# The feed-forward layers of a two-layer encoder in float32r: later sends, two swapped products, a later SiLU

## The chip, the cores and the metric

The kernel runs on one core of one Trainium2 chip, as one program. The metric is the device time of an execution in microseconds; the time of the kernel before is the median of three runs. The profile comes from one further execution, taken by the hardware profiler.

## The reference

The whole trunk of an encoder is computed for 1024 positions of width 1024: a gated delta-rule layer, a feed-forward layer, a chunked attention layer that reads a shared key and value, a second feed-forward layer, and a last norm. The change touches only the two feed-forward layers:

```python
FFN_DIM = 2816
FFN_CONV = 3

def conv_ffn(xn, w_up, conv_w, conv_b, w_down):
    h = causal_dwconv(xn @ w_up, conv_w) + conv_b
    gate, val = h[..., :FFN_DIM], h[..., FFN_DIM:]
    return (jax.nn.silu(gate) * val) @ w_down
...
h = h + conv_ffn(rmsnorm(h, f_norm[layer]), f_w_up[layer], f_conv[layer], f_conv_b[layer], f_w_down[layer])
```

## The kernel before

**Float32 from two halves.** A float32 operand is cut into a rounded high part and the rest. ScalarE (ACT) rounds (`cut_high`, L1434: tiles `uh`, `dh`, `eh`), and GpSimd (POOL) or VectorE (DVE) subtracts to get the low part (`cut_low`, L1412: `ul`, `dl`, `el`). A product of two such operands is three matmuls (`triple`: L1446 high by high, L1447 and L1448 with a low part of one side). A step of the program is one product of four `triple`s: twelve matmuls of 128x512.

**Seven products for eight.** Both matrix products are computed two by two blocks at a time by a scheme with seven block products in place of eight, so VectorE also makes sums of blocks of weights (`r<-r,r`, `ay<-a,a`) and of activations. The hidden width is 22 tiles of 128 for the gate and 22 for the value. Tile `j` of the first matrix takes the products `(j, n)` with `n` from 1 to 7, which write a PSUM bank `pu`. Products 1 and 2 of a tile share a bank: after `(j, 1)` ScalarE copies the bank to `keep` (L1575), and `(j, 2)` accumulates into the same bank. The x operands are `xh` and `xl` (products 1, 2, 3), `x7`, `xt2` (product 6), `xt1` (product 5) and `xt4`. Tile 0 is computed by eight plain products.

**The second matrix** takes the hidden tiles two at a time, in nine groups `g` of seven products, `second(g, n)`, in the order n = 1, 2, 5, 3, 6, 7, 4, one for every two products of the first matrix. Each writes two PSUM banks `pd`. `drain(g, n)` takes the banks out: by ScalarE copies to tiles `stage` (L1802), or for n = 6, 7 by VectorE sums onto the stage of products 3 and 5. `send(g, n)` (L1817) then adds the two stage tiles to a sum in device memory by two accumulating DMAs that GpSimd issues; products 3 and 5 have no send of their own. Product 1 goes to a shared sum `d_e`, which belongs into three of the four quarters. At the end of a layer `load_e` fetches the shared sum, half `u` at a time, and `send_e(u, n)` (L1824) adds it to the quarters of n = 6, 7 and 4.

**Convolution.** `taps` applies three taps per tile: step 0 on ScalarE (L1538), steps 1 and 2 on VectorE (L1541). `silu(j)` (L1544) is ScalarE's, `gated(j)` is VectorE's product with the value.

**What sets the order.** Within `ffn` nothing is scheduled by a tool: the order of instructions on every engine is written out. `step` appends a product to the list `seq`. `at(i, f, rank)` hangs a job on step `i`; before each step its jobs are run in order of rank, and what they issue stands in this order on each engine's queue.

```python
for i in range(len(seq) + 8):
    for _, f in sorted(jobs.pop(i, ()), key=lambda j_: j_[0]):
        f()
    if i < len(seq):
        seq[i]()
```

An operand of the first matrix is cut two steps ahead of its product (rank 1 where no other is given; on POOL where no engine is given). The weights of the second matrix are cut three steps ahead with rank 1.2, its hidden tiles with 1.4. The table `H` holds steps and ranks for the start of a layer: `first` is the order of the first 15 products behind tile 0, and `conv` gives step and rank of the taps, the SiLU (`s`) and the gated product (`m`) of tiles 0 to 2.

Of the kernel before, what the change touches and what calls it, by code (L numbers as in the profile page):

```python
# [28 lines left out]
def trunk_kernel(  # L29
# [25 lines left out]
    o = 0  # L55
# [452 lines left out]
    with ExitStack() as ph:  # L508
# [137 lines left out]
        def heads(t):  # L646

            return t // 2, range(4 * (t % 2), 4 * (t % 2) + 4)
# [602 lines left out]
        h, late = [], None  # L1251
# [92 lines left out]
        xh, xl = act_tiles()  # L1344
# [6 lines left out]
        with tc.manual_schedule(engines={mybir.EngineType.PE, mybir.EngineType.DVE, mybir.EngineType.Activation}):  # L1351
# [4 lines left out]
            for t in range(4):  # L1356
                s, hds = heads(t)
# [49 lines left out]
    def ffn(layer, h, hp, xs, tail, d_r, last):  # L1407
# [16 lines left out]
        H = {'cut': ({(0, 1): (0, 0), (1, 0): (1, 0), (1, 1): (1, 1)}, {(0, 1): (0, 0), (1, 0): (0, 0), (1, 1): (1, 0)}), 'c0': ({(0, 0): 'gg', (0, 1): 'av', (1, 0): 'av', (1, 1): 'ag'}, {(0, 0): 'gg', (0, 1): 'gg', (1, 0): 'gg', (1, 1): 'ag'}), 'x': {('s', 7): (5, 1), ('h', 7): (6, 1.306), ('s', 6): (5, 1.466), ('h', 6): (6, 2.01), ('l', 7): (7, 2.004), ('l', 6): (7, 2.612), ('s', 5): (9, 2), ('h', 5): (9, 2.01), ('l', 5): (10, 2.406), ('s', 4): (11, 2), ('h', 4): (11, 2.918), ('l', 4): (12, 1.039)}, 'xl': {7: (), 6: (), 5: (), 4: ()}, 'beats': ({(0, 2): 1, (1, 0): 20}, {(1, 3): 1, (2, 0): 20}), 'first': [(1, 1), (1, 2), (2, 1), (1, 7), (2, 2), (1, 6), (1, 5), (2, 7), (1, 4), (1, 3), (2, 6), (2, 5), (2, 4), (2, 3), (3, 1)], 'o': (2, 3, 5, 7, 7, 9, 11), 'ops': {(3, 3): (0.5, 2.5, 'v'), (3, 4): (1, 2, 'v'), (3, 2): (0.5, 1.12, 'v'), (1, 3): (1.1, 3, 'v'), (2, 7): (1, 3, 'g'), (2, 6): (1.1, 2.5, 'g'), (1, 5): (1, 1.3, 'v'), (3, 7): (0.5, 1.7, 'v'), (2, 1): (0.5, 2.5, 'v'), (3, 5): (1, 3, 'g'), (3, 6): (1.1, 1.12, 'g')}, 'conv': {0: {'g0': (11, 3.208), 'v0': (12, 1.815), 'v1': (13, 2), 'v2': (14, 2.418), 'g1': (14, 0.401), 'g2': (15, 2.01), 's': (16, 0.011), 'm': (17, 2)}, 1: {'v0': (18, 1.304), 'v1': (18, 1.468), 'v2': (19, 2), 'g0': (19, 0.403), 'g1': (20, 0.913), 'g2': (21, 0.903), 's': (22, 1.6), 'm': (23, 1.311)}, 2: {'v0': (22, 1.164), 'v1': (25, 1.805), 'v2': (25, 2), 'g0': (24, 2.606), 'g1': (26, 0.906), 'g2': (27, 0.408), 's': (28, 1.6), 'm': (30, 1.805)}}, 'gp': {1: (18, 1.807), 2: (24, 1.602)}, 'mix': (0, 1)}  # L1424

        seq, jobs = [], {}

        def at(i, f, rank=1):

            jobs.setdefault(max(i, 0), []).append((rank, f))  # L1430

        def cut_high(src, ring, copy=nc.scalar.copy):
            hi, lo = [(wd if ring == "e" else wf).tile([P, HALF], F32R, name=ring + x, tag=ring + x, bufs=RINGS[ring]) for x in "hl"]
            copy(hi, src)  # L1434
            return hi, lo
# [9 lines left out]
        def triple(ps, w, x, cw, first, last):  # L1445
            mm(ps, w[0][:, cw], x[0], start=first, stop=False, skip_group_check=True)  # L1446
            mm(ps, w[0][:, cw], x[1], start=False, stop=False, skip_group_check=True)  # L1447
            mm(ps, w[1][:, cw], x[0], start=False, stop=last, skip_group_check=True)  # L1448
# [62 lines left out]
        def operand(j, n, lo=True):  # L1511
# [110 lines left out]
        def plain(i):  # L1622
            def f():
# [18 lines left out]
        due = {}  # L1642
        for c, (j, n) in enumerate(plan):
# [65 lines left out]
        v0, v1, v2, g0, g1, g2 = [(v, i) for v in (1, 0) for i in range(3)]  # L1709
# [60 lines left out]
        def channels(g, n):  # L1770
            b11, b12, b21, b22 = [conv_t[2 * g + k, 1][:, hs(s)] for k in range(2) for s in range(2)]
            if n == 5:
                tt(nc.vector, b11, b12, b11, sub)
            elif n == 6:
                tt(nc.vector, b11, b22, b11, sub)
            elif n == 7:
                tt(nc.vector, b12, b22, b12, sub)
            elif n == 4:
                tt(nc.vector, b21, b21, b11, sub)
            src = {1: b11, 2: b21, 5: b11, 3: b22, 6: b11, 7: b12, 4: b21}[n]  # L1780
            bops[g, n] = cut_high(src, "e")
# [24 lines left out]
        def total(n, u):  # L1806
            if n == 1:
                return d_e[u]
            c, s = where[n]
            return d_c[c, s, u]  # L1810

        def send(g, n):
            for u in range(2):
                if g == 0 and (layer == 1 or n == 1):
                    nc.sync.dma_start(out=total(n, u), in_=stage[g, n, u])
                else:
                    nc.gpsimd.dma_start(out=total(n, u), in_=stage[g, n, u], accum_op=add)  # L1817
# [5 lines left out]
        def send_e(u, n):  # L1823
            nc.gpsimd.dma_start(out=total(n, u), in_=stage["e", u], accum_op=add)  # L1824

        for g in range(NG):
            p_ = {n: pos["d", g, n] for n in ORDER}
            b_ = {n: pos["d", g - 1, n] for n in ORDER} if g else {1: p_[1] - 4, 3: p_[1] - 4, 7: p_[1] - 4, 4: p_[1] - 3}
            for q, n in ((11, 7), (12, 3), (21, 7), (22, 4)):
                at(b_[n] - 2, lambda g=g, q=q: load_a(g, q), 3 + q / 100)  # L1830
            for n in ORDER:
                if n == 3:

                    def third(g=g):
                        low = channels(g, 3)
                        weights(g, 3, low)

                    at(p_[n] - 3, third, 1.2)
                else:
                    at(p_[n] - 3, lambda g=g, n=n: weights(g, n), 1.2)  # L1840
                    at(p_[n] - 3, lambda g=g, n=n: channels(g, n), 1.4)
                at(p_[n] + 1, lambda g=g, n=n: drain(g, n), 0)
                if n not in (3, 5):
                    at(p_[n] + 2, lambda g=g, n=n: send(g, n), 0.5)

        for u, i in ((0, pos["d", NG - 1, 5]), (1, fin_at + 2)):
            at(i, lambda u=u: load_e(u), 3)
            for k, n in enumerate((6, 7, 4)):
                at(i + 2 + k // 2, lambda u=u, n=n: send_e(u, n), 0.6)


        k0 = 2 * NG
# [25 lines left out]
        for q in range(8):  # L1878
            i = (fin_at + 1, fin_at + 1, pos[FP - 2, 6], pos[FP - 2, 7], pc[0], pc[3], pc[1], pc[1])[q]
# [59 lines left out]
        else:  # L1939
# [108 lines left out]
            i = 8  # L2048
# [34 lines left out]
    xh, xl = xb  # L2083
# [7 lines left out]
    first = two_tiles([load_w(w_kv, 0, fold=g_kv, on_act=True), load_w(b_w_q, 0, fold=g_b, on_act=True)], tail0, next_tile)  # L2091
# [5 lines left out]
    with ExitStack() as ph:  # L2097
# [354 lines left out]
        h, tails = [], []  # L2452
# [271 lines left out]
```

## Time and profile before

| | |
|---|---|
| median of 3 runs | 2499.43 us (2498.5 to 2502.1) |
| span of the profiled execution, first to last instruction | 2493.3 us |
| median less the span | 6.1 us |
| PE (matmuls) busy | 2466.1 us, 99% of the span |
| DVE, POOL, ACT busy | 1842.5, 1523.0, 1442.1 us |
| first feed-forward layer | about 643 to 1295 us |
| second feed-forward layer | about 1833 to 2480 us |

Matmul rows overlap: a row lasts 0.39 us, and the next one begins 0.23 us after the last began. So the busy share says little, and a loss is read from the starts of two successive matmuls, less 0.23 us each. The profiled execution has a span alone and no device time of its own beside it; the median of the runs shown is 6.1 us over this span.

### The profile page before, as it was taken

To read this page: it belongs to the slowest core of one execution; us is meant where nothing else is said; L and a number is where in the kernel's file an instruction comes from. 1 tells how busy PE (TensorE), PEld (TensorE's weight loads), DVE (VectorE), ACT (ScalarE), POOL (GpSimd) and SP (SyncE) were. 2 spreads that over 40 slices of the span, in tenths; PEclk is the share of its full clock that TensorE was granted. 3 is DMA by queue.
4 is the path that set the end of the run, shared out by engine and by line. 5 is a ranking of instruction groups with operands and counts; after the bars stand their busy time and mean duration, and the time that the engine had idled before them with its cause. 6 is when DMAs were issued, how large, how long until landed. Compare 5 with 4: busy or idle time off the path is not lost.

```text
span 2493.3 us, 39279 instructions
## 1 busy us (share of the span) xinstructions
PE 2466.1 (99%) x13785; PEld 2057.0 (83%) x13785; DVE 1842.5 (74%) x2985; ACT 1442.1 (58%) x2770; POOL 1523.0 (61%) x1548
## 2 busy tenths in 40 slices
PE   8999999999999999999999999999999999999998
PEld 6888888888888888888788888888877888888877
DVE  5665874567798888888866656666589788888886
ACT  6444546474465556565555666667456565666555
POOL 3655653357357777777626454455554777778774
PEclk9999999999999999999999999999999999999999
DMA  8734435565347777777841232333444799777788
GB/s 228 188 105 118 142 110 153 156 194 163 96 108 148 150 153 151 153 144 156 183 151 55 67 80 77 81 76 95 145 114 119 184 176 180 166 169 171 152 187 224
DMA packets 383877, 353.19 MB, mean 142 GB/s; under 512 B 97600, under 2 KB 304448, under 8 KB 383680
## 3 DMA queue, kind: packets, MB, share of 16 engines
q1 hardware_dynamic: 350704, 243.46, 34.4%
q0 software_dynamic: 28224, 98.58, 22.5%
q10 hardware_dynamic: 4752, 8.65, 0.9%
q8 instruction: 108, 1.77, 0.3%
q14 instruction: 89, 0.73, 0.1%
HBM read 182.25 MB, written 156.30 MB: 136 GB/s over the span
## 4 chain that ended last, share of the span: by engine, by line
PE 81%; POOL 6%; DVE 4%; issue 4%; DMA 2%; ACT 2%; SPq 0%; ACTq 0%; POOLq 0%; DVEq 0%
PE acc L118 8%; PE pu L1448 8%; PE acc L119 8%; PE acc L120 8%; PE pu L1446 8%; PE pu L1447 8%; PE pd L1448 3%; PE pd L1446 3%; PE pd L1447 3%; POOL ul L1412 3%; PE acco L118 2%; PE acco L120 2%; PE acco L119 2%; PE ptp L2353 2%; PE poT L2399 1%
## 5 line engine op out<-in xcount | busy, mean ns | idle before, releaser
L1412 POOL TENSOR_TENSOR ul<-r,uh 128x512 fp32r<-128x512 f32 x266 | 430.4, 1638 | 258.3 <-ACT uh L1434 253.5
L118 PE MATMUL acc<-xh,whi 128*128 128x512 f32 x896 | 369.3, 413 | 0.5 <-ACT xh L1094 0.5
L119 PE MATMUL acc<-xl,whi 128*128 128x512 f32 x896 | 352.1, 393 | 0.4 <-POOL xl L381 0.3
L120 PE MATMUL acc<-xh,wlo 128*128 128x512 f32 x896 | 351.3, 392 | 0.0
L103 POOL TENSOR_TENSOR wlo<-wraw,whi 128x256 fp32r<-128x256 f32 (+1 forms) x326 | 237.0, 758 | 107.8 <-ACT whi L101 105.3
L1434 ACT CAST uh<-r 128x512 fp32r<-128x512 f32 x289 | 177.1, 623 | 183.3 <-DVE r L1412 148.8
L1448 PE MATMUL pu<-xh,ul 128*128 128x512 f32 x524 | 204.4, 390 | 0.7 <-POOL ul L1412 0.7
L1446 PE MATMUL pu<-xh,uh 128*128 128x512 f32 x524 | 204.4, 390 | 0.7 <-ACT keep L1575 0.7
L1802 ACT COPY stage<-pd 128x1024 f32<-128x1024 f32 x180 | 175.3, 1014 | 49.7 <-PE pd L1448 48.8
L1447 PE MATMUL pu<-xl,uh 128*128 128x512 f32 x524 | 203.9, 389 | 0.0
L120 PEld LDWEIGHTS acc<-xh,wlo 128*128 128x128 f32 x896 | 168.5, 188 | 37.1
L2308 POOL TENSOR_SCALAR sS<-sS,st 128x640 f32<-128x640 f32 (+4 forms) x128 | 87.6, 691 | 178.4 <-DVE st L2306 168.2
L119 PEld LDWEIGHTS acc<-xl,whi 128*128 128x128 f32 x896 | 169.3, 189 | 28.4 <-POOL xl L381 2.5
L118 PEld LDWEIGHTS acc<-xh,whi 128*128 128x128 f32 x896 | 169.1, 189 | 27.5 <-ACT xh L1094 0.9
L1412 POOL TENSOR_TENSOR dl<-a,dh 128x512 fp32r<-128x512 f32 x90 | 153.3, 1703 | 47.4 <-ACT dh L1434 37.2
L1541 DVE SCALAR_TENSOR_TENSOR gate<-gpre,colt,gate 128x1023 f32<-128x1023 f32 (+2 forms) x92 | 176.5, 1919 | 2.5 <-ACT gate L1538 1.8
L1541 DVE SCALAR_TENSOR_TENSOR val<-vpre,colt,val 128x1023 f32<-128x1023 f32 x88 | 149.2, 1696 | 29.3 <-ACT val L1538 29.3
L2298 DVE CUSTOM_DVE_ANT_0 sS<-sc,bt 128x640 f32<-128x640 f32 (+4 forms) x128 | 84.1, 657 | 111.4 <-PE sc L2294 75.9
L1412 DVE TENSOR_TENSOR r<-r,r 128x512 f32<-128x512 f32 x160 | 130.3, 814 | 32.8 <-POOL ul L1412 31.7
L1412 DVE TENSOR_TENSOR el<-val,eh 128x512 fp32r<-128x512 f32 x90 | 85.4, 949 | 43.2 <-ACT eh L1434 43.2
L1448 PEld LDWEIGHTS pu<-xh,ul 128*128 128x128 f32 x524 | 98.4, 188 | 22.8 <-POOL ul L1412 1.4
L1446 PEld LDWEIGHTS pu<-xh,uh 128*128 128x128 f32 x524 | 98.4, 188 | 21.1 <-ACT keep L1575 1.1
(428 smaller groups left out, 7197.9 us busy)
## 6 DMA issues: line engine op xcount, KB each, us to landing
r<-in_f_w_up_dram SPq DMA_DIRECT2D x176, 256.0 KB, 4.5
d_r<-stage POOLq DMA_DIRECT2D x78, 512.0 KB, 8.1
d_c<-stage POOLq DMA_DIRECT2D x70, 512.0 KB, 8.4
a<-in_f_w_down_dram SPq DMA_DIRECT2D x72, 256.0 KB, 2.9
wraw<-in_a_w_in_dram SPq DMA_DIRECT2D x32, 512.0 KB, 4.5
d_e<-stage POOLq DMA_DIRECT2D x32, 512.0 KB, 8.3
wraw<-in_a_w_out_dram SPq DMA_DIRECT2D x16, 512.0 KB, 4.1
d_r<-h ACTq DMA_DIRECT2D x32, 256.0 KB, 2.8
```

Source lines behind the costliest of these rows:

```text
L103: nc.gpsimd.tensor_tensor(lo[:, c], raw[:, c], hi[:, c].bitcast(F32), op=ALU.subtract)
L118: mm(ps, hi[:, kw, wcol : wcol + P], rh[k][s], start=st, stop=False)
L119: mm(ps, hi[:, kw, wcol : wcol + P], rl[k][s], start=False, stop=False)
L120: mm(ps, lo[:, kw, wcol : wcol + P], rh[k][s], start=False, stop=sp)
L1412: tt = lambda eng, o, a, b, op: eng.tensor_tensor(o, a, b, op=op)
L1434: copy(hi, src)
L1446: mm(ps, w[0][:, cw], x[0], start=first, stop=False, skip_group_check=True)
L1447: mm(ps, w[0][:, cw], x[1], start=False, stop=False, skip_group_check=True)
L1448: mm(ps, w[1][:, cw], x[0], start=False, stop=last, skip_group_check=True)
L1541: nc.vector.scalar_tensor_tensor(t_[:, a:c1], p_[:, a - step : c1 - step], w[:, 2 - step : 3 - step], t_[:, a:c1], op0=ALU.mult, op1=ALU.add)
L1802: nc.scalar.copy(t_, ps)
L2308: nc.gpsimd.tensor_scalar(S, S, st[:, 3:4], 1.0, op0=ALU.mult, op1=ALU.mult)
```

## The change

Four edits in `ffn`, which is called for both layers. In the table `H` two entries change: in `first` the products (1, 2) and (2, 1) change places, and in `conv` the SiLU of tile 0 keeps its step, 16, but its rank goes from 0.011 to 1.55, behind the rounding of an operand (rank 1.1) in the same step. The send of product 2 of a group gets rank 1.06 for 0.5, behind the cut of an operand with rank 1 in its step. The sends of the shared sum get rank 1.5 for 0.6, behind all cuts of their step. Nothing is added or removed.

```diff
-        H = {... 'first': [(1, 1), (1, 2), (2, 1), (1, 7), (2, 2), ...], 'conv': {0: {... 's': (16, 0.011), 'm': (17, 2)}, ...
+        H = {... 'first': [(1, 1), (2, 1), (1, 2), (1, 7), (2, 2), ...], 'conv': {0: {... 's': (16, 1.55), 'm': (17, 2)}, ...
...
                 if n not in (3, 5):
-                    at(p_[n] + 2, lambda g=g, n=n: send(g, n), 0.5)
+                    at(p_[n] + 2, lambda g=g, n=n: send(g, n), 1.06 if n == 2 else 0.5)
...
             for k, n in enumerate((6, 7, 4)):
-                at(i + 2 + k // 2, lambda u=u, n=n: send_e(u, n), 0.6)
+                at(i + 2 + k // 2, lambda u=u, n=n: send_e(u, n), 1.5)
```

On POOL, in the second group of the first layer (and so in eight groups of each layer; the first group's row stays): `r21` is the operand of product 6, `r11` that of product 5 of the same tile, and `d_r0000`, `d_r0001` are the two halves of a quarter of the output.

```order
 L1412 TENSOR_TENSOR dl_8698<-ay_8695,dh_8697 128x512
+L1412 TENSOR_TENSOR ul_8742<-r21_8490,uh_8741 128x512
 L1817 DMA d_r0000_87<-stage_8718 128x1024
 L1817 DMA d_r0001_88<-stage_8720 128x1024
-L1412 TENSOR_TENSOR ul_8744<-r21_8490,uh_8743 128x512
 L1412 TENSOR_TENSOR ul_8765<-r11_8533,uh_8764 128x512
 L1412 TENSOR_TENSOR dl_8775<-a12_8375,dh_8774 128x512
```

The two sends stood ahead of both low parts of products 6 and 5; now they stand between the two.

On POOL, in the last group of the first layer, with the first half of the shared sum (the last three sends; `r12` and `r22` are operands of the first matrix, `dl` and `el` belong to the second):

```order
 L1412 TENSOR_TENSOR dl_12240<-a12_11769,dh_12239 128x512
+L1412 TENSOR_TENSOR ul_12283<-r12_12140,uh_12282 128x512
 L1824 DMA d_r0010_89<-stage_12243 128x1024
 L1824 DMA d_r0110_93<-stage_12243 128x1024
-L1412 TENSOR_TENSOR ul_12285<-r12_12140,uh_12284 128x512
+L1412 TENSOR_TENSOR ul_12307<-r22_12049,uh_12306 128x512
+L1412 TENSOR_TENSOR dl_12312<-ay_12160,dh_12311 128x512
+L1412 TENSOR_TENSOR el_12317<-val_11642,eh_12316 128x512
 L1824 DMA d_r0100_91<-stage_12243 128x1024
-L1412 TENSOR_TENSOR ul_12308<-r22_12049,uh_12307 128x512
-L1412 TENSOR_TENSOR dl_12313<-ay_12160,dh_12312 128x512
-L1412 TENSOR_TENSOR el_12318<-val_11642,eh_12317 128x512
```

Each send now stands behind the low parts of its step: the first two behind one, the third behind three more. For the second half of the sum the third send moves behind one low part.

On ACT, at step 16 of the first layer: `r21` is the operand of product (2, 6), and the rows behind it those of (2, 5) and (2, 4).

```order
 L1434 CAST uh_8002<-r12_7624 128x512
+L1434 CAST uh_8021<-r21_7796 128x512
 L1544 ACT_TABLE_LOAD
 L1544 ACTIVATE gate_7918<-gate_7918 128x1024
-L1434 CAST uh_8022<-r21_7796 128x512
 L1434 CAST uh_8042<-r11_7622 128x512
 L1434 CAST uh_8063<-r22_7823 128x512
```

The rounding of (2, 6) now stands ahead of the table load and the SiLU, the other two stay behind them. On DVE the swapped products change only which operand the first and which the second of two cuts is for.

More of the change, by code (lines that the diff above doesn't have):

```diff
@@ L1423, in ffn @@
         RINGS = dict(u=3, d=2, e=2)
-        H = {'cut': ({(0, 1): (0, 0), (1, 0): (1, 0), (1, 1): (1, 1)}, {(0, 1): (0, 0), (1, 0): (0, 0), (1, 1): (1, 0)}), 'c0': ({(0, 0): 'gg', (0, 1): 'av', (1, 0): 'av', (1, 1): 'ag'}, {(0, 0): 'gg', (0, 1): 'gg', (1, 0): 'gg', (1, 1): 'ag'}), 'x': {('s', 7): (5, 1), ('h', 7): (6, 1.306), ('s', 6): (5, 1.466), ('h', 6): (6, 2.01), ('l', 7): (7, 2.004), ('l', 6): (7, 2.612), ('s', 5): (9, 2), ('h', 5): (9, 2.01), ('l', 5): (10, 2.406), ('s', 4): (11, 2), ('h', 4): (11, 2.918), ('l', 4): (12, 1.039)}, 'xl': {7: (), 6: (), 5: (), 4: ()}, 'beats': ({(0, 2): 1, (1, 0): 20}, {(1, 3): 1, (2, 0): 20}), 'first': [(1, 1), (1, 2), (2, 1), (1, 7), (2, 2), (1, 6), (1, 5), (2, 7), (1, 4), (1, 3), (2, 6), (2, 5), (2, 4), (2, 3), (3, 1)], 'o': (2, 3, 5, 7, 7, 9, 11), 'ops': {(3, 3): (0.5, 2.5, 'v'), (3, 4): (1, 2, 'v'), (3, 2): (0.5, 1.12, 'v'), (1, 3): (1.1, 3, 'v'), (2, 7): (1, 3, 'g'), (2, 6): (1.1, 2.5, 'g'), (1, 5): (1, 1.3, 'v'), (3, 7): (0.5, 1.7, 'v'), (2, 1): (0.5, 2.5, 'v'), (3, 5): (1, 3, 'g'), (3, 6): (1.1, 1.12, 'g')}, 'conv': {0: {'g0': (11, 3.208), 'v0': (12, 1.815), 'v1': (13, 2), 'v2': (14, 2.418), 'g1': (14, 0.401), 'g2': (15, 2.01), 's': (16, 0.011), 'm': (17, 2)}, 1: {'v0': (18, 1.304), 'v1': (18, 1.468), 'v2': (19, 2), 'g0': (19, 0.403), 'g1': (20, 0.913), 'g2': (21, 0.903), 's': (22, 1.6), 'm': (23, 1.311)}, 2: {'v0': (22, 1.164), 'v1': (25, 1.805), 'v2': (25, 2), 'g0': (24, 2.606), 'g1': (26, 0.906), 'g2': (27, 0.408), 's': (28, 1.6), 'm': (30, 1.805)}}, 'gp': {1: (18, 1.807), 2: (24, 1.602)}, 'mix': (0, 1)}
@@ new lines, in ffn @@
+        H = {'cut': ({(0, 1): (0, 0), (1, 0): (1, 0), (1, 1): (1, 1)}, {(0, 1): (0, 0), (1, 0): (0, 0), (1, 1): (1, 0)}), 'c0': ({(0, 0): 'gg', (0, 1): 'av', (1, 0): 'av', (1, 1): 'ag'}, {(0, 0): 'gg', (0, 1): 'gg', (1, 0): 'gg', (1, 1): 'ag'}), 'x': {('s', 7): (5, 1), ('h', 7): (6, 1.306), ('s', 6): (5, 1.466), ('h', 6): (6, 2.01), ('l', 7): (7, 2.004), ('l', 6): (7, 2.612), ('s', 5): (9, 2), ('h', 5): (9, 2.01), ('l', 5): (10, 2.406), ('s', 4): (11, 2), ('h', 4): (11, 2.918), ('l', 4): (12, 1.039)}, 'xl': {7: (), 6: (), 5: (), 4: ()}, 'beats': ({(0, 2): 1, (1, 0): 20}, {(1, 3): 1, (2, 0): 20}), 'first': [(1, 1), (2, 1), (1, 2), (1, 7), (2, 2), (1, 6), (1, 5), (2, 7), (1, 4), (1, 3), (2, 6), (2, 5), (2, 4), (2, 3), (3, 1)], 'o': (2, 3, 5, 7, 7, 9, 11), 'ops': {(3, 3): (0.5, 2.5, 'v'), (3, 4): (1, 2, 'v'), (3, 2): (0.5, 1.12, 'v'), (1, 3): (1.1, 3, 'v'), (2, 7): (1, 3, 'g'), (2, 6): (1.1, 2.5, 'g'), (1, 5): (1, 1.3, 'v'), (3, 7): (0.5, 1.7, 'v'), (2, 1): (0.5, 2.5, 'v'), (3, 5): (1, 3, 'g'), (3, 6): (1.1, 1.12, 'g')}, 'conv': {0: {'g0': (11, 3.208), 'v0': (12, 1.815), 'v1': (13, 2), 'v2': (14, 2.418), 'g1': (14, 0.401), 'g2': (15, 2.01), 's': (16, 1.55), 'm': (17, 2)}, 1: {'v0': (18, 1.304), 'v1': (18, 1.468), 'v2': (19, 2), 'g0': (19, 0.403), 'g1': (20, 0.913), 'g2': (21, 0.903), 's': (22, 1.6), 'm': (23, 1.311)}, 2: {'v0': (22, 1.164), 'v1': (25, 1.805), 'v2': (25, 2), 'g0': (24, 2.606), 'g1': (26, 0.906), 'g2': (27, 0.408), 's': (28, 1.6), 'm': (30, 1.805)}}, 'gp': {1: (18, 1.807), 2: (24, 1.602)}, 'mix': (0, 1)}
```

## The prediction

> **What bounds the kernel now.** I read the page first, then who waited for whom, then the timeline of each engine where a moved row stands.
>
> ```profile
> span 2493.3 us, 39279 instructions
> PE 2466.1 (99%) x13785; PEld 2057.0 (83%) x13785; DVE 1842.5 (74%) x2985; ACT 1442.1 (58%) x2770; POOL 1523.0 (61%) x1548
> ```
>
> The matmuls bound the kernel, and no edit changes their number. All that can be won or lost is the time in which PE stands still. The waits of PE and of its weight load, in total, number and longest, that lie at the moved rows:
>
> ```profile
> PEld pu L1448 <- POOL ul L1412: 13.3, 20, 1.5
> PE pd L1446 <- ACT stage L1802: 1.7, 2, 0.9
> PEld pul L1446 <- ACT keep L1603: 1.1, 2, 0.6
> PEld pul L1448 <- POOL ul L1412: 0.4, 1, 0.4
> ```
>
> So the stake is small: some waits of under a microsecond for a low part from POOL, one per group of products, and two drains. What one such wait costs PE, in the third group of the first layer:
>
> ```profile
> 836.99 0.39 PE L1447 MATMUL pu<-xt2l,uh 128*128 128x512 f32 x1
> 837.55 0.50 PE L1448 MATMUL pu<-xt2h,ul 128*128 128x512 f32 x1 [0.17 <-POOL ul L1412]
> 840.42 0.39 PE L1448 MATMUL pu<-xt1h,ul 128*128 128x512 f32 x1
> ```
>
> The next matmul should come 0.23 after 836.99 and comes 0.56 after it: 0.33 lost, and 0.11 more since the late matmul is 0.50 long where others are 0.39. So 0.44 in such a group. The third row is the first need of the next low part, for product 5.
>
> **Sends of product 2.** The engines around that wait:
>
> ```profile
> 831.00 1.75 POOL L1412 TENSOR_TENSOR dl<-ay,dh 128x512 fp32r<-128x512 f32 x1
> 832.69 1.77 POOL L1817 DMA_DIRECT2D d_r<-stage  x2
> 835.17 4.04 POOL L1412 TENSOR_TENSOR ul<-r,uh 128x512 fp32r<-128x512 f32 x2 [0.71 <-ACT uh L1434]
> ...
> 831.52 2.31 DVE L1541 SCALAR_TENSOR_TENSOR val<-vpre,colt,val 128x1022 f32<-128x1022 f32 x1
> 833.75 1.41 DVE L1412 TENSOR_TENSOR r<-r,r 128x512 f32<-128x512 f32 x2
> 835.07 1.28 DVE L1541 SCALAR_TENSOR_TENSOR gate<-gpre,colt,gate 128x1023 f32<-128x1023 f32 x1
> ...
> 834.46 0.62 ACT L1434 CAST uh<-r 128x512 fp32r<-128x512 f32 x1 [0.47 <-DVE r L1412]
> ```
>
> The sends stand just ahead of the first low part, but they do not hold it up. They end at 834.46; POOL then idles 0.71 until the rounding ends at 835.08. That waits for VectorE's sum, and the sum for a tap that took 2.31 where another takes 1.28, because POOL's `dl` ran beside it until 832.75. The two sums then run at 0.70 each beside the sends, so a send does not slow VectorE. And the low part itself lasts till 837.50 because a tap began 0.1 ahead of it. In an earlier group, where the rounding came sooner, the low part starts while its sends still run (to 747.00):
>
> ```profile
> 745.25 1.75 POOL L1817 DMA_DIRECT2D d_r<-stage  x2
> 746.59 4.03 POOL L1412 TENSOR_TENSOR ul<-r,uh 128x512 fp32r<-128x512 f32 x2
> ```
>
> So what the edit takes away from the first wait is bounded by 0.44 and 0, and I take 0.
>
> What it adds is that the second low part now stands behind two sends. Where a low part with its input ready stands behind two sends:
>
> ```profile
> 880.79 1.77 POOL L1817 DMA_DIRECT2D d_e<-stage  x2
> 881.96 1.92 POOL L1412 TENSOR_TENSOR ul<-r,uh 128x512 fp32r<-128x512 f32 x1
> ```
>
> From the first send's start to the low part's end (883.88) it is 3.09. In the new place the first send starts as the first low part ends, a little before 837.50, say 837.46, and the second low part ends at 840.55 instead of 839.21. PE started 0.05 after a low part's end at 837.55, so it can go on at 840.60; it wants the part at 840.42. That is 0.18 late, and with the refill of 0.11 a loss of 0.29. There are eight such groups in each layer; the first of the second layer shows no wait here, so I count 15: +4.3. The cover that hides the rest of the 1.34 is the slack of the second low part (839.21 to 840.37). The bounds are nothing, if 0.2 more is hidden, and 0.8 a group (the second rival below). The sends also land 4.8 later, and the next drain writes the stage tiles that they read:
>
> ```profile
> 847.10 1.92 ACT L1802 COPY stage<-pd 128x1024 f32<-128x1024 f32 x2
> d_r<-stage POOLq DMA_DIRECT2D x78, 512.0 KB, 8.1
> ```
>
> The second copy (848.0) waits for the second send, issued at about 838.05 and landing 8.1 later, at 846.2: just in time, so nothing.
>
> A rule to weigh here: the Trainium skill, "SBUF — State Buffer", section "SBUF: two separate sides", says that VectorE and GpSimd take a shared port in turn for a whole instruction, and warns that a GpSimd DMA cannot write its descriptors while VectorE holds it in a two-port mode. The first half agrees with the 2.31 above. If the warning held for VectorE's sums too, the sends, now beside three of them, would take some 0.6 longer a group, and the sum would be 9 us worse; the rows 1.77 and 1.75, both beside VectorE's work, speak against it, and I leave it out.
>
> **Sends of the shared sum.** The last group of the first layer:
>
> ```profile
> 1187.71 1.77 POOL L1824 DMA_DIRECT2D d_r<-stage  x2
> 1191.97 2.24 POOL L1412 TENSOR_TENSOR dl<-ay,dh 128x512 fp32r<-128x512 f32 x1
> ...
> 1190.84 3.93 DVE L1412 TENSOR_TENSOR r<-r,r 128x512 f32<-128x512 f32 x1 [2.12 <-POOL ul L1412]
> ...
> 1195.78 0.39 PE L1448 MATMUL pu<-xt4h,ul 128*128 128x512 f32 x1
> 1198.05 0.40 PE L1448 MATMUL pd<-eh,dl 128*128 128x512 f32 x1
> ```
>
> VectorE's sum waits for the low part behind the first two sends, and is then shut out (3.93 for 0.68) until `dl` ends at 1194.2. Behind it stand the hidden tile's rounding, the drain on ACT and the product `pd`: three matmul steps take 2.27 for 0.69, so 1.58 is lost. With the low part ahead of the sends the sum can run at about 1189.4 and end before POOL's next low part begins; the drain moves some 4 us forward, and the whole 1.58 goes. In the second layer the same wait for the drain stands (1.7 in two above) without most of the wait that follows: I take 1.3. For the second half, the third send blocks POOL for 4.3 us until an older send lands:
>
> ```profile
> 1231.40 0.86 POOL L1824 DMA_DIRECT2D d_r<-stage  x1 [4.32 <-DMA d_r<-stage]
> ```
>
> The low part now passes it: of the load waits 0.4 and 1.1 (two), 0.23 each is prefetch, and 0.11 each comes on top, so 0.3 and 0.9. In all -4.1; the bounds are 0 and -4.1. I take -4.0. What is late next is the third send of the first half itself: it now issues at about 1194.7 rather than 1190.1, and its buffer is wanted again at about 1200, which I expect it just to make.
>
> **Swapped products.** In the first layer (1, 2) accumulates into the bank of (1, 1) and waits for the copy `keep`:
>
> ```profile
> 670.18 0.39 PE L1448 MATMUL pu<-xh,ul 128*128 128x512 f32 x1
> 671.24 0.50 PE L1446 MATMUL pu<-xh,uh 128*128 128x512 f32 x1 [0.68 <-ACT keep L1575]
> ...
> 692.82 0.68 DVE L1412 TENSOR_TENSOR ul<-r,uh 128x512 fp32r<-128x512 f32 x1
> 693.59 0.47 PE L1448 MATMUL pu<-xh,ul 128*128 128x512 f32 x1
> ```
>
> 1.06 for 0.23 and the refill: 0.94 goes, since (2, 1) has a bank of its own and its operand is cut in the place of the other. But VectorE works without a gap through this stretch and sets the pace: its low part of (1, 3) ends at 693.50 and PE needs it at 693.59. PE arrives earlier and waits there. The gain is between 0.94 and 0; by that row 0.1. In the second layer plain products already stand between the two, so 0.
>
> **SiLU of tile 0.**
>
> ```profile
> 692.46 1.28 ACT L1544 ACT_TABLE_LOAD   x1
> 694.72 1.88 ACT L1434 CAST uh<-r 128x512 fp32r<-128x512 f32 x3
> ...
> 693.43 0.68 DVE L1412 TENSOR_TENSOR r<-r,r 128x512 f32<-128x512 f32 x1
> 697.77 2.14 DVE L1541 SCALAR_TENSOR_TENSOR val<-vpre,colt,val 128x1023 f32<-128x1023 f32 x1 [0.73 <-ACT val L1538]
> 700.27 1.42 DVE L1412 TENSOR_TENSOR keep<-pu,keep 128x512 f32<-128x512 f32 x2 [0.36 <-PE pu L1448]
> 710.57 0.68 DVE L1412 TENSOR_TENSOR ul<-r,uh 128x512 fp32r<-128x512 f32 x1
> ...
> 697.63 0.50 PE L1448 MATMUL pu<-xt2h,ul 128*128 128x512 f32 x1 [1.06 <-POOL ul L1412]
> 711.41 0.39 PE L1448 MATMUL pu<-x7h,ul 128*128 128x512 f32 x1
> ```
>
> Product (2, 6) loses 1.06 of idleness, 1.3 with overlap and refill. The rounding can begin only when the sum of 693.43 ends, at 694.1, so it moves forward by 0.6, and its low part escapes VectorE's gated product: most of the 1.3 goes. But the table load and the SiLU now wait for 694.8 and end at 697.1, 2.3 later; the tap on ACT behind them starts 1.6 later (one of three roundings is out of its way), VectorE's tap at 699.4, and the sums of `keep` at 700.55 for 700.27. From there VectorE goes on almost without a gap to the low part of (3, 7), which ends at 711.25 against 711.41. So PE wins 1.2 at (2, 6), and at (3, 7) stands where it stood, plus 0.28 at the worst. Between -1.2 and +0.3; by the chain of rows +0.28, in both layers +0.6.
>
> The Trainium skill, "ScalarE: Activation LUTs", section "What ACT_TABLE_LOAD costs", adds a drain of about 1.4 us to a load of 1.28. By it the SiLU would end later still and the sum be up to 2.8 worse. The row agrees with the load alone, and the SiLU follows it at once here.
>
> **Sum.** -0.1 + 0.6 + 4.3 - 4.0 = +0.8 on the span of 2493.3, which lies 6.1 under the median: 2500.2.
>
> **Rivals.**
> *The sends do hold up the low parts.* For it: they stand last ahead of them. Against it: the idle 0.71 and the group at 745. Then 15 times 0.44 goes and nothing comes: -6.6 - 4.0 + 0.5 = -10.1, 2489.3. Chance 0.14.
> *VectorE is shut out in each group (slower).* In the row 1190.84 a sum waited through POOL instructions that followed a send without a gap. In the new place `ul` and `dl` follow the sends in the same way, and VectorE's `el` (0.68) and a tap would wait for both, some 2 us, until the drain at 847.1 comes late for its product. It decides when that delay exceeds the drain's slack of about 2.1; past it, 0.5 a group more: 7.5, 2507.7. Against it: the delay is by my rows just under the slack. Chance 0.17.
> *The sends are hidden in their new place.* Slack covers 1.16 of the 1.34 already; with 0.2 less PE loses nothing there: 2495.9. Chance 0.18.
> *The shared sum gives nothing back*, for its third send lands late for the next user of its buffer: 2504.2. Chance 0.1.
>
> **How the numbers follow.** My case, 2500.2, has the rest, 0.41. A measurement of this kernel can tell about 0.2%, 5 us, from no change. The first rival is faster (0.14, and 0.02 of the third); the second is slower, and half of the fourth: 0.22. The rest, 0.62, is the same. The range leaves out the best of the first rival (all bounds together: 2485.4) and the worst of the second: 2491.5 to 2508; my case's own is 2496 to 2504.
>
> **What the changed profile would show.** PE's load waits for POOL's `ul` in the regular groups stay, at L1448 of `xt2h`, and as many come at `xt1h`; if the total of 13.3 falls below 8, I was wrong on the sends. The 3.93 of VectorE and the drain's waits in the last groups go. The wait for `keep` at 670 goes, while PE stands still before 693.6 instead. (2, 6) loses its wait and (3, 7) gets one. It goes wrong if a low part that I hold for bound by VectorE was bound by the send, or if a delay of VectorE passes through a drain to PE.

## The result and the profile after

The changed kernel took 2520.24 us (median of 4 runs, 2519.26 to 2520.48) against 2500.14 for the kernel before on the same chip: a ratio of 1.0078, 95% interval 1.0066 to 1.0090. It is slower by 20 us. The forecast was 2500.2, no change, with a range from 2491.5 to 2508. Of all the executions timed for this document one ran in a slow state, 3945.58 us, one of twelve of the kernel "sends moved, second low part on VectorE" below, and the ratios leave it out.

The first lines of the page after, and then those waits of PE (and of its weight load, PEld) that are new or changed: in total, number, longest.

```profile
span 2518.6 us, 39250 instructions
PE 2478.9 (98%) x13785; PEld 2054.0 (82%) x13785; DVE 1862.2 (74%) x2985; ACT 1441.3 (57%) x2770; POOL 1518.2 (60%) x1548
```

```profile
PE pu L1448 <- POOL ul L1412: 6.3, 19, 0.7
PE pd L1447 <- POOL dl L1412: 5.0, 8, 0.7
PE pd L1448 <- POOL dl L1412: 3.7, 8, 0.5
PE pm L862 <- issue: 2.2, 1, 2.2
...
PEld pu L1448 <- POOL ul L1412: 25.4, 45, 1.1
```

The matmuls are as many as before; PE stands still longer. The load's waits for `ul` went from 13.3 (20) to 25.4 (45), PE's own from 4.6 (9) to 6.3 (19). The two rows for `dl` have no counterpart before: sixteen waits for `dl`, the low part of the weights of the second matrix, eight in each layer, one in each group whose sends moved. No term of the forecast was about `dl`.

Where the time lies is read from the starts of PE's matmuls. A group is measured here from the first matmul of its product 1 to that of the next group (fourth group of the first layer: 875.33 to 932.80 before, 882.19 to 941.03 after, 57.47 and 58.84). Summed over the profiled executions:

| stretch | after less before, us |
|---|---|
| before the first feed-forward layer, untouched | +2.9 |
| start of the layers, up to the second matrix | +0.5 and +0.4 |
| eight groups with moved sends, first layer | +11.5 |
| the same, second layer | +10.8 |
| products of the last tile (shared sum, second half) | -0.8 and -0.5 |
| all else | +0.5 |

The 2.9 ahead of the first layer holds the 2.2 of the row `pm`; in the executions of all the kernels below this stretch lies between 643.1 and 649.7, whatever was changed, so it is a difference between executions. So, it seems, is about 1.1 of the 11.5: the first of its groups takes 57.63 in the kernel before, but 58.7 to 58.8 in four kernels below that leave the sends of product 2 where they were. Left are 21 us, close to the 20 of the runs, and 1.36 for a regular group.

**A group after the change**, the fourth of the first layer: POOL, VectorE, ScalarE and PE, on their timelines (start, us, engine, line, operation, what it waited for).

```profile
899.76 2.33 POOL L1412 TENSOR_TENSOR ul<-r,uh 128x512 fp32r<-128x512 f32 x1 [2.42 <-ACT uh L1434]
902.04 1.80 POOL L1817 DMA_DIRECT2D d_r<-stage  x2
903.19 1.96 POOL L1412 TENSOR_TENSOR ul<-r,uh 128x512 fp32r<-128x512 f32 x1
906.45 2.21 POOL L1412 TENSOR_TENSOR dl<-a,dh 128x512 fp32r<-128x512 f32 x1 [1.29 <-ACT dh L1434]
...
900.87 1.77 DVE L1412 TENSOR_TENSOR ay<-ay,a 128x512 f32<-128x512 f32 x1
902.67 3.04 DVE L1412 TENSOR_TENSOR a<-a,ay 128x512 f32<-128x512 f32 x1
910.12 0.69 DVE L1412 TENSOR_TENSOR r<-r,r 128x512 f32<-128x512 f32 x1 [0.49 <-POOL ul L1412]
...
905.75 0.62 ACT L1434 CAST dh<-a 128x512 fp32r<-128x512 f32 x1 [4.76 <-DVE a L1412]
...
904.77 0.39 PE L1447 MATMUL pu<-xt1l,uh 128*128 128x512 f32 x1
905.21 0.50 PE L1448 MATMUL pu<-xt1h,ul 128*128 128x512 f32 x1
907.86 0.39 PE L1447 MATMUL pd<-el,dh 128*128 128x512 f32 x1
908.71 0.50 PE L1448 MATMUL pd<-eh,dl 128*128 128x512 f32 x1 [0.47 <-POOL dl L1412]
```

The sends follow the first low part without a gap, and the second low part ends at 905.15, 3.11 after the first send began (3.09 was forecast). PE gets it 0.21 late (905.21 less 904.77 less 0.23), and with the refill 0.32 is lost; 0.29 was forecast. But VectorE's sum `a` does not run beside the sends either. It begins at 902.67, lasts 3.04 where such a sum takes 0.68, and ends 0.56 after the second low part. Behind `a` stand the rounding `dh`, which waited 4.76, POOL's `dl`, and PE's matmul with it: 0.62 late, 0.73 with the refill. In the second layer `dl` is used one matmul earlier, and the loss there is 0.97.

The same places in a group of the kernel before:

```profile
838.08 1.67 DVE L1412 TENSOR_TENSOR a<-a,ay 128x512 f32<-128x512 f32 x1
844.16 0.69 DVE L1412 TENSOR_TENSOR r<-r,r 128x512 f32<-128x512 f32 x1 [0.49 <-POOL ul L1412]
...
840.48 2.23 POOL L1412 TENSOR_TENSOR dl<-a,dh 128x512 fp32r<-128x512 f32 x1 [1.28 <-ACT dh L1434]
...
842.91 0.39 PE L1447 MATMUL pd<-el,dh 128*128 128x512 f32 x1
843.14 0.39 PE L1448 MATMUL pd<-eh,dl 128*128 128x512 f32 x1
```

PE did not wait for `dl` there (843.14 less 842.91 is 0.23), and `a` ended at 839.75, 2.25 after the first low part (837.50); now at 905.71, 3.62 after it (902.09). From the end of `a` to the sum `r`, which waits for the low part behind `dl`, it is 4.41 in both kernels. So everything behind `a` moved by the same 1.37, and a group became 1.36 longer: 0.32 at `xt1`, 0.73 at `dl`, and most of the rest at `xt2`, where the wait of the fourth group grew from 0.22 to 0.43.

**The last groups of the first layer after the change**: POOL, VectorE, ScalarE, PE.

```profile
1204.29 1.78 POOL L1824 DMA_DIRECT2D d_r<-stage  x2
1205.43 1.94 POOL L1412 TENSOR_TENSOR ul<-r,uh 128x512 fp32r<-128x512 f32 x1
1206.69 1.93 POOL L1412 TENSOR_TENSOR dl<-ay,dh 128x512 fp32r<-128x512 f32 x1
1211.40 0.88 POOL L1824 DMA_DIRECT2D d_r<-stage  x1
...
1204.38 0.69 DVE L1412 TENSOR_TENSOR r<-r,r 128x512 f32<-128x512 f32 x1 [0.49 <-POOL ul L1412]
1204.99 4.18 DVE L1412 TENSOR_TENSOR val<-val 128x512 f32<-128x512 f32 x1
...
1217.12 1.24 ACT L1538 ACTIVATE val<-vpre,colt 128x1024 f32<-128x1024 f32 x1 [2.90 <-DMA d_r<-stage]
...
1222.56 0.39 PE L1447 MATMUL pu<-x7l,uh 128*128 128x512 f32 x1
1223.28 0.50 PE L1448 MATMUL pu<-x7h,ul 128*128 128x512 f32 x1 [0.33 <-POOL ul L1412]
```

The sum `r`, 3.93 long before, now takes 0.69. The next one on VectorE, `val`, is shut out in its place for 4.18, until `dl` ends at 1208.62. And the third send, issued at 1211.40, lands just ahead of 1217.12, where ScalarE's first tap of tile 19 has waited 2.90 for it: the tap writes the buffer that the send reads. PE pays at `x7`, 0.49 and the refill, and at the product after it, 0.46 with the refill.

**The start of a layer**: PE at product (3, 7), ScalarE at the SiLU.

```profile
713.68 0.39 PE L1447 MATMUL pu<-x7l,uh 128*128 128x512 f32 x1
714.66 0.50 PE L1448 MATMUL pu<-x7h,ul 128*128 128x512 f32 x1 [0.59 <-DVE ul L1412]
...
697.86 1.28 ACT L1544 ACT_TABLE_LOAD   x1
699.16 1.06 ACT L1544 ACTIVATE gate<-gate 128x1024 f32<-128x1024 f32 x1
```

### The profile page after: what moved, and what is told of

It reads as the page before. It is cut to its first block, busy times and chain, and to the rows that moved or that the text cites. A ratio compares the mean times of both kernels' runs of the same rounds, so it can differ in the third digit from the quotient of the medians.

```text
span 2518.6 us, 39250 instructions
## 1 busy us (share of the span) xinstructions
PE 2478.9 (98%) x13785; PEld 2054.0 (82%) x13785; DVE 1862.2 (74%) x2985; ACT 1441.3 (57%) x2770; POOL 1518.2 (60%) x1548
## 4 chain that ended last, share of the span: by engine, by line
PE 75%; DVE 7%; POOL 7%; issue 6%; ACT 3%; DMA 1%; SPq 0%; POOLq 0%; ACTq 0%; DVEq 0%
PE acc L118 8%; PE acc L119 8%; PE acc L120 8%; PE pu L1448 6%; PE pu L1446 6%; PE pu L1447 6%; PE pd L1448 3%; PE pd L1447 3%; POOL ul L1412 3%; PE pd L1446 3%; PE acco L118 2%; PE acco L120 2%; PE acco L119 2%; PE ptp L2353 2%; POOL dl L1412 2%
## 5 line engine op out<-in xcount | busy, mean ns | idle before, releaser
L1412 DVE TENSOR_TENSOR r<-r,r 128x512 f32<-128x512 f32 x160 | 122.9, 768 | 29.5 <-POOL ul L1412 28.3
L1434 ACT CAST dh<-a 128x512 fp32r<-128x512 f32 x90 | 55.7, 619 | 108.8 <-DVE a L1412 108.6
```

The lines of the kernel that those rows point to most:

```text
L1412: tt = lambda eng, o, a, b, op: eng.tensor_tensor(o, a, b, op=op)
```

## The experiments

The theory after this comparison: the sends push the second low part by 1.34, VectorE's sum `a` ends behind that low part, and `dl` behind `a` has no reserve. All lengths below are from the profiled executions, in us, first layer and second layer; "group" is the median of the six intervals between the third and the ninth group, "last" the stretch from the last group's start to its last product, "tile" the products of the last tile. A group without a stall takes 57.12 (252 matmuls). The ratio is that to the kernel before, run on the same chip.

| kernel | ratio, 95% interval | group | last | tile |
|---|---|---|---|---|
| before | 1 | 57.50, 57.78 | 53.60, 53.33 | 22.30, 22.02 |
| the change | 1.0078 (1.0066 to 1.0090) | 58.86, 59.15 | 54.93, 54.81 | 21.53, 21.53 |
| sends of product 2 alone | 1.0092 (1.0077 to 1.0107) | 58.87, 59.19 | 55.13, 54.73 | 21.83, 23.08 |
| the change without these | 0.9999 (0.9991 to 1.0008) | 57.48, 57.81 | 53.33, 53.45 | 21.53, 21.53 |
| swap and SiLU alone | 1.0002 (0.9993 to 1.0011) | 57.49, 57.75 | 53.51, 53.31 | 22.32, 22.63 |
| shared sum, second half alone | 0.9996 (0.9988 to 1.0005) | 57.49, 57.74 | 53.49, 53.29 | 21.53, 21.53 |
| no sends of product 2 | 0.9997 (0.9987 to 1.0007) | 57.50, 57.71 | 53.58, 53.37 | 21.55, 21.89 |
| sends behind both low parts | 1.0019 (1.0008 to 1.0030) | 57.70, 57.86 | 53.87, 53.36 | 22.33, 23.04 |
| one of the two sends moved | 1.0032 (1.0021 to 1.0043) | 57.95, 58.24 | 54.25, 53.79 | 21.61, 22.52 |
| sends moved, second low part on VectorE | 0.9978 (0.9970 to 0.9987) | 57.13, 57.35 | 52.79, 52.65 | 21.55, 22.35 |
| second low part on VectorE alone | 0.9986 (0.9978 to 0.9995) | 57.13, 57.32 | 52.63, 52.60 | 22.54, 23.06 |
| that, and the second half | 0.9974 (0.9965 to 0.9982) | 57.15, 57.53 | 52.70, 52.58 | 21.53, 21.53 |
| shared sum, no third send in the first half | 0.9993 (0.9985 to 1.0002) | 57.49, 57.71 | 52.20, 52.64 | 21.53, 21.53 |
| the change, second low part on VectorE | 0.9982 (0.9973 to 0.9991) | 57.15, 57.33 | 52.55, 52.45 | 21.53, 21.53 |

**Which edit costs the time.** First the edits by themselves, all against the kernel before (the second is the changed kernel with one line put back):

```diff
-                    at(p_[n] + 2, lambda g=g, n=n: send(g, n), 0.5)
+                    at(p_[n] + 2, lambda g=g, n=n: send(g, n), 1.06 if n == 2 else 0.5)
```

> Only the sends of product 2 are given rank 1.06; the other three edits are left out. Theory (the sends delay the second low part and, through VectorE's sum a, the low part dl of product 3): the whole loss of the groups is here, 15 to 16 groups of about 1.35 each, so +20 to +22 us on the kernel before, near 2521. The PE waits for dl (16, about 0.6 to 0.9 each) and for the second ul are all there. Rival (the loss in the groups needs the other edits, the shared sum above all, or comes partly from elsewhere): +10 us or less, and no dl waits or fewer than 8.

> The changed kernel with the sends of product 2 back at rank 0.5; the other three edits stay. Theory: the groups cost what they did before, the start of each layer costs 0.4 more, the second half of the shared sum wins 0.8 and 0.5, the first half nothing: -0.5, within 1.5 us of the kernel before. No wait for dl of over 0.2 in the groups. Rival (the swapped products, the SiLU or the shared sum carry a part of the 20 us): +3 us or more. My recorded terms would make it -3.5.

The line alone makes the kernel slower by 0.92% by the ratio (medians 2522.39 and 2498.05), with the sixteen waits for `dl`; without it the three other edits together change nothing that can be measured. The theory holds, and no other edit has a part in the loss.

> Only the swapped products and the later SiLU of tile 0. By the segments of the changed run: +0.4 in each layer, +0.8 us in all, which the timing can hardly tell from nothing. My recorded terms: +0.5. Rival (the 2.9 us that the changed run lost ahead of the first layer belongs to these edits): +3 to +4 us.

```diff
-                at(i + 2 + k // 2, lambda u=u, n=n: send_e(u, n), 0.6)
+                at(i + 2 + k // 2, lambda u=u, n=n: send_e(u, n), 1.5 if u else 0.6)
```

> The kernel before, with the sends of the shared sum at rank 1.5 in the second half alone; the first half stays at 0.6. Theory (the low parts pass a send that is held up by an older one's landing): the segment of the last tile's products gets 0.8 shorter in the first layer and 0.5 in the second, -1.3 us in all; nothing else moves. Rival (the sends only move to a later collision): 0 or slower.

Swap and SiLU: no change that the runs can tell; the start of the layers is 0.4 and 0.3 longer, much as in the changed kernel. In the second layer this is clear (73.0 in every kernel without the two edits, 73.3 to 73.6 with them); in the first the two overlap (69.9 to 70.6, and 70.4 to 70.9). The second half of the shared sum shortens the last tile to 21.53 in both layers. Every kernel with this edit has 21.53, while those without it lie between 21.55 and 23.08: the edit takes away a wait that differs from execution to execution. In the runs 1.3 us is too little to be told.

**Were the low parts held up by the sends before?** The sends of product 2 left out in the groups:

```diff
-                    at(p_[n] + 2, lambda g=g, n=n: send(g, n), 0.5)
+                    at(p_[n] + 2, lambda g=g, n=n: send(g, n), 0.5) if n != 2 or g == 0 else None
```

> The kernel before without the sends of product 2 in groups 1 to 8 (that addition is missing from the totals). It tells whether the sends held up the first low part in the old place. Theory (the first low part waits for VectorE's sum, not for the sends): the 0.33 and 0.11 at the first low part stay in the groups, and the time is that of the kernel before, 0 to -1.5 us. Rival (my recorded first rival, that the sends hold it up): the wait goes, 15 times 0.44, -6.6 us, POOL's ul starts ahead of VectorE's tap.

POOL and PE in the fourth group of this kernel:

```profile
895.14 4.04 POOL L1412 TENSOR_TENSOR ul<-r,uh 128x512 fp32r<-128x512 f32 x2 [2.41 <-ACT uh L1434]
...
897.07 0.39 PE L1447 MATMUL pu<-xt2l,uh 128*128 128x512 f32 x1
897.53 0.50 PE L1448 MATMUL pu<-xt2h,ul 128*128 128x512 f32 x1
```

POOL now idles 2.41 for the rounding where it idled 0.7 behind the sends, and PE still waits (0.23 and the refill). The time is the same. In their old place the sends cost nothing, since they ran while POOL had nothing to do; my first rival is out.

**Dose and place.** One of the two sends moved (`send(g, n, us)` sends the halves in `us`), and both moved further:

```diff
-                    at(p_[n] + 2, lambda g=g, n=n: send(g, n), 0.5)
+                    at(p_[n] + 2, lambda g=g, n=n: send(g, n, (0,)), 0.5)
+                    at(p_[n] + 2, lambda g=g, n=n: send(g, n, (1,)), 1.06 if n == 2 else 0.5)
```

> The kernel before with only the second of the two sends of product 2 moved behind the first low part; the first stays in its old place. Half the dose. Theory (a slack has to be used up first): one send pushes the second low part by about 0.45 instead of 1.33, so xt1 does not wait (its slack was 1.16) and dl, whose slack was 0.4 in the first layer and 0.2 in the second, comes 0.1 and 0.3 late plus the refill: 0.2 and 0.4 a group, +4 to +6 us. Rival (each send costs the same, whatever the slack): half of the 24 us of the full move, +12 us.

```profile
894.76 2.32 POOL L1412 TENSOR_TENSOR ul<-r,uh 128x512 fp32r<-128x512 f32 x1 [1.58 <-ACT uh L1434]
897.03 0.88 POOL L1817 DMA_DIRECT2D d_r<-stage  x1
897.64 1.60 POOL L1412 TENSOR_TENSOR ul<-r,uh 128x512 fp32r<-128x512 f32 x1
...
897.66 2.13 DVE L1412 TENSOR_TENSOR a<-a,ay 128x512 f32<-128x512 f32 x1
904.20 0.69 DVE L1412 TENSOR_TENSOR r<-r,r 128x512 f32<-128x512 f32 x1 [0.49 <-POOL ul L1412]
```

`a` ends 2.71 after the first low part, 0.46 later than before, and a group is 0.45 longer. PE does not wait at `xt1`, and `dl` is 0.10 late in the first layer and 0.31 in the second, as expected. But a group loses more than these waits, since the wait at `xt2` grows too (0.41 for 0.22 in the group shown). By the ratio it is 8.0 us (5.2 to 10.7): above my 4 to 6, which the interval just reaches, and under the rival's 12. By the lengths of the groups I was wrong that a slack of 0.4 has to be used up first: the delay of `a` passes into the group's length whole. From the end of `a` to `r` it is 4.41 here too.

```diff
-                    at(p_[n] + 2, lambda g=g, n=n: send(g, n), 0.5)
+                    at(p_[n] + 2 + (n == 2), lambda g=g, n=n: send(g, n), 1.1 if n == 2 else 0.5)
```

> The kernel before with the sends of product 2 behind both low parts, ahead of product 3's dl (one step later, rank 1.1). Theory (the loss is the 1.34 by which the sends push the second low part, and with it VectorE's a and product 3's dl): the second low part and a stand where they stood, the sends run while POOL waited for dh anyway (839.2 to 840.9, where dh comes at 840.4), dl starts at most 0.5 later, and the groups cost 0 to 0.3 more each: 0 to +4 us on the kernel before, no wait at xt1, waits for dl 0.3 at most. Rival (sends beside VectorE's sums shut VectorE out wherever they stand, or dl is held as the low part was): dl waits of 0.5 and over stay, +8 us or more.

```profile
899.04 4.03 POOL L1412 TENSOR_TENSOR ul<-r,uh 128x512 fp32r<-128x512 f32 x2 [2.42 <-ACT uh L1434]
903.01 1.81 POOL L1817 DMA_DIRECT2D d_r<-stage  x2
904.36 2.22 POOL L1412 TENSOR_TENSOR dl<-a,dh 128x512 fp32r<-128x512 f32 x1
...
901.95 1.67 DVE L1412 TENSOR_TENSOR a<-a,ay 128x512 f32<-128x512 f32 x1
...
855.48 1.01 ACT L1802 COPY stage<-pd 128x1024 f32<-128x1024 f32 x1 [1.56 <-DMA d_r<-stage]
```

`a` takes 1.67 again, the waits for `dl` are gone, and a group costs 0.2 and 0.1 more than before. By the ratio it is 4.7 us (2.0 to 7.5), a little above the 0 to 4 that I gave and under the rival's 8. The rest is not at `dl`, which begins 1.29 after the second low part's end (903.07), where it was 1.27. It is in some groups alone. Of the six regular groups of the first layer three are as long as before (57.44, 57.51, 57.59), and three are longer by 0.6, 0.3 and 0.4. The last row, from the group before the one shown, is one cause: the sends now land so late that the drain of product 3, which writes the stage tiles that they read, waits for them. Such waits of over 1 us stand in the first and the last of these three groups, and the second follows such a group; the kernel before and the changed kernel have none.

**What holds `a` off.** The sends moved as in the change, and the second low part cut on VectorE, so that no POOL instruction that is ready stands behind the sends:

```diff
+                if n == 5 and j > 3 and j % 2:
+                    low = []
+                    at(i - 2, lambda j=j, n=n, low=low: low.append(operand(j, n, False)), 1)
+                    at(i - 2, lambda low=low: low[0](nc.vector), 1.1)
+                else:
+                    at(i - 2, lambda j=j, n=n: operand(j, n), 1)
```

> Only the sends of product 2 moved as in the changed kernel, but the second low part of these groups is cut on VectorE behind the gate's tap, so that no POOL instruction that is ready stands behind the sends (dl still waits for its rounding). It asks what shut VectorE's sum a out for 3.0. Theory (a low part that is ready behind the sends holds VectorE off from then on; sends alone don't): ul, ay and a take 0.7 to 1.8 each beside the sends, a ends before it did, no waits for dl or at xt1: -1 to +2 us on the kernel before. Rival (the sends themselves hold VectorE off): the sum that meets the sends takes 2 or more, dl comes about 0.8 late a group: +8 to +15 us.

```profile
892.48 2.33 POOL L1412 TENSOR_TENSOR ul<-r,uh 128x512 fp32r<-128x512 f32 x1 [2.42 <-ACT uh L1434]
894.76 1.80 POOL L1822 DMA_DIRECT2D d_r<-stage  x2
897.48 2.17 POOL L1412 TENSOR_TENSOR dl<-a,dh 128x512 fp32r<-128x512 f32 x1 [0.93 <-PE pu L1447]
...
893.58 1.78 DVE L1412 TENSOR_TENSOR ul<-r,uh 128x512 fp32r<-128x512 f32 x1
895.28 0.68 DVE L1412 TENSOR_TENSOR ay<-ay,a 128x512 f32<-128x512 f32 x1
896.00 0.69 DVE L1412 TENSOR_TENSOR a<-a,ay 128x512 f32<-128x512 f32 x1
901.10 0.69 DVE L1412 TENSOR_TENSOR r<-r,r 128x512 f32<-128x512 f32 x1 [0.16 <-POOL ul L1412]
```

Beside the same two sends (894.76 to 896.56) the sums take 0.68 and 0.69, where `a` took 3.04 with a ready low part behind the sends. So the sends do not shut VectorE out; the POOL instruction behind them does, once it is ready, and already while the sends run. `a` now ends 1.88 after the first low part, 0.37 earlier than before, and a group is 0.37 and 0.43 shorter. With the other kernels this gives four points in the first layer: `a` moved by -0.37, 0, +0.46 and +1.37, the group by -0.37, 0, +0.45 and +1.36. (The first point lies at the length without a stall, 57.12, under which no group can fall, so it is the other three that show the proportion.) The time falls to 2493.0, 0.2% under the kernel before, which is more than I expected: the wait at `xt2` goes too in most groups. From the end of `a` to `r` it is 4.41 once more.

Two controls with the same cut: without the moved sends, and in the changed kernel with all its edits.

> The kernel before with the second low part of groups 1 to 8 cut on VectorE, and the sends of product 2 in their old place. With the run that moved them too (2493.0) it tells what the move costs when no ready low part stands behind it. Theory: nothing, so 2492 to 2494.5 here too, 5 us under the kernel before, and no waits at xt2 in most groups. Rival (the move itself gained the 5 us once its cost was gone): this one stays at the kernel before, 2497 to 2499.

> The changed kernel, all four edits, with one thing more: the second low part of groups 1 to 8 is cut on VectorE, so that no ready POOL instruction stands behind the moved sends. Theory (the whole loss hangs on that low part behind the sends): the 22 us go and 4 to 5 more, as in the runs with that cut (2493.0 and 2496.2); the shared sum's second half gives 1.3, the start of the layers takes 0.8: about 2494, a ratio of 0.998 to the kernel before, the groups 57.1 to 57.9 long, and no wait for dl in them. Rival (the other edits add to the loss once the groups are tight): 2500 or more.

Without the move the groups have the same length (57.13 and 57.32 for 57.13 and 57.35), so the move costs nothing where no ready low part stands behind it, and it gains nothing. The runs alone do not settle this: the kernel took 2496.23, 3.5 us under the kernel before by the ratio (1.2 to 5.5) where I expected 5, and the intervals with and without the move overlap. With all four edits and this cut the kernel takes 2494.99 instead of 2520.24, 0.9982 of the kernel before instead of 1.0078: one low part on another engine takes away the whole loss.

> The same with the shared sum's sends of the second half at rank 1.5 as well: a version that may beat both kernels. If the two add, 1.3 us under the one without it: 2491.5, 6.5 under the kernel before. Rival (the last groups' timing has moved and the sends collide elsewhere): no better than the one without, 2493.

2493.13 against 2499.68, 0.9974: the lowest ratio of all, though its interval overlaps with those of the kernels without the second half, so the runs do not show that the two gains add up. It beats both the kernel before and the changed one.

**The first half of the shared sum.** Its third send left out, with the other sends at rank 1.5 (that addition is missing from one total):

```diff
-                at(i + 2 + k // 2, lambda u=u, n=n: send_e(u, n), 0.6)
+                at(i + 2 + k // 2, lambda u=u, n=n: send_e(u, n), 1.5) if u or n != 4 else None
```

> The kernel before with the shared sum's sends at rank 1.5, and without the third send of the first half (that addition is missing from one total). Theory (in the changed kernel the third send lands at 1216.96, the tile's first tap on ACT writes its buffer and waits 2.9 for that, and x7 and xt2 wait behind it): the waits at x7 and xt2 go in both layers, 1.1 and 1.25 less than in the changed kernel's tail, so -3.5 us on the kernel before in all, of which -1.3 is the second half. Rival (POOL's own order behind the moved sends makes these waits): they stay, -1.3 us.

```profile
1202.61 1.26 ACT L1538 ACTIVATE val<-vpre,colt 128x1024 f32<-128x1024 f32 x1
```

The tap of tile 19 no longer waits. The stretch of the last group is 1.40 and 0.69 shorter than before, while with the third send (the change without the sends of product 2) it is 0.27 shorter and 0.12 longer. So the landing of the third send took back what the earlier drain gave. In the second layer only the wait at `x7` goes, and that at `xt2`, 0.46 with the refill, stays: there my theory gave too much to the landing. With the second half it is 3.3 by the trace for 3.5 expected; the ratio, -1.7 us (-3.7 to +0.5), agrees but can't show it alone.

## Why the prediction was wrong

**The step that failed** is in the term for the sends of product 2: "The cover that hides the rest of the 1.34 is the slack of the second low part (839.21 to 840.37)." The delay was followed to one reader, PE at `xt1`, and there it was right: 0.29 forecast, 0.32 measured. It was not followed to the second one, VectorE, whose `a` already ended behind that low part in the kernel before (the row of 1.67), and from there to `dh`, `dl` and product 3. That chain had no reserve, and the term was 0.29 a group where it is 1.36: 4.3 us forecast, 21 measured by the traces and 23 (19 to 27) by the ratio of the kernel with this edit alone. The upper bound of 0.8 a group fell with it, and so did the range. With 21 for 4.3, -1.4 for the -4.0 of the shared sum and +0.8 for +0.5 the sum would have been +20, as measured.

**The second rival** had the mechanism, VectorE shut out in each group, but named `el` and the drain as the victims and set its price at 0.5 a group past a slack. The victim is `a`, and there is no slack.

**The first low part** is not held by the sends: right, shown by the kernel without sends. **The landing** of the moved sends is in time for the next drain: no wait for it shows, though the second send of the group shown landed at 911.28, 8.7 after its issue where 8.1 was taken. The reserve is small: issued some 1.8 us later in the group, behind both low parts, they do hold up drains.

**The shared sum, -4.0 forecast.** The second half was right in kind: -1.2 forecast, -0.8 and -0.5 measured. The first half failed at "which I expect it just to make": the drain's waits mostly went, 1.58 and 1.27 down to 0.34 and 0.08 in the change without the sends of product 2. But waits at `x7` and `xt2` of 1.07 and 1.26 came, of which the third send's landing made 1.07 and 0.84. The fourth rival said this. `val` is also still shut out, as `r` was, by the two POOL instructions behind the sends.

**Swap and SiLU, +0.5 forecast, +0.8 measured** in the changed execution. As said, the wait for `keep` goes and PE stands still a little before the products up to (1, 3) instead, (2, 6) loses most of its wait (1.22 down to 0.10) and (3, 7) gets one: 0.75 and the refill, more than my 0.28. Another, 0.30 and the refill, comes at (2, 5), which I had not seen.

**The rules weighed there.** The Trainium skill, "SBUF — State Buffer", section "SBUF: two separate sides", warns of sends whose descriptors cannot be written while VectorE runs in a two-port mode. Beside VectorE's sums no such stop shows: the pairs of sends shown took 1.75 to 1.81 in all these kernels, so leaving it out was right. The same section of the Trainium skill says that the one of the two engines that starts first has the shared port for a whole instruction. By the starts of the rows, `a` (902.67) should then have had the port ahead of the low part (903.19), and it waited all the same, 3.04. But the starts of POOL's rows are rough, and no run shows when the low part took the port: if it did so as soon as it could be handed to POOL, behind the first low part's end at 902.09, the rule holds. The Trainium skill, "ScalarE: Activation LUTs", section "What ACT_TABLE_LOAD costs", has a drain of about 1.4 on top of the load: the load ends at 699.14 and the SiLU begins at 699.16, so it does not show here either.

## What to carry to other kernels

A delay on one queue must be followed to all who wait for it, through one engine that holds off another as much as through semaphores: here the reader that was priced lost 0.3 us a group, and an engine that had only stood behind the same instruction lost the other 1.0. The issue of an accumulating DMA cost nothing here where the next instruction on its queue wasn't ready anyway, as long as the DMA landed in time, and most of its length where that one was ready (1.36 of 1.80 for two sends). And before a kernel with short waits is reordered, ask whether the chain is already closed: if each group waits a little in the same place, a slack inside the group may not hide a delay; here it hid none.

## What was not expected of the hardware

A POOL instruction that is ready holds VectorE off while the DMA issues ahead of it on POOL's queue still run: 3.04 and 4.18 us for sums that take 0.68, against 0.69 with an instruction behind the sends that wasn't ready. The low part takes 1.30 alone (`ul`, 908.79 to 910.09 in the changed kernel) and ended at 905.15, so it can hardly have run before the sends ended at 903.84; `a`, begun at 902.67, would have ended at 903.35. That the low part takes a port that both need at its dispatch is how I read this; no run shows the moment itself.

Moving a subtraction from POOL to VectorE made VectorE's busy time smaller, 1823.9 us in the kernel with that alone for 1842.5, with sixteen instructions more: its rows are shorter by more than the new ones take (`ay` 0.68 for 1.78, `a` 0.69 for 1.67).
